# Two groups of attention heads as one pipeline beside a block-wise projection, with a new block order

## The chip, the cores and the metric

The kernel runs on one core of one Trainium2 chip. The metric is device time in microseconds (us), smaller is better. A core has TensorE (PE in the profile; PEld is its weight load), VectorE (DVE), ScalarE (ACT), GpSimd (POOL) and SyncE (SP), which issues the DMAs here. The program hands each engine a queue of instructions.

## The reference, cut to what matters

One step of a two-layer backbone on 1152 tokens (9 tiles of 128: tile 0 is the context, tiles 1 to 8 are latent). The even layer, of which the changed part computes the inputs and one branch:

```python
def even_layer(x, shift, scale, gate, norm_pre, norm_post, w_out, w_in, sink, ..., ctx):
    h = rms_norm(x, norm_pre) * (1.0 + scale) + shift
    qa, ka, va, ga, pb, gb = split_cols(h @ w_in, [...])
    ya = gqa_window_latent(apply_rope(qa), apply_rope(ka), va, k_ctx, v_ctx, sink)   # mixer A
    yb, _ = rwkv_mix(pb, ...)                                                        # mixer B
    y = concat([ya * silu(ga), yb * silu(gb)]) @ w_out
    return x + gate * rms_norm(y, norm_post)
```

Mixer A has two groups of four query heads that share one key and value head. A latent tile attends to the 128 cached context tokens and to a window of itself and the tile on either side, with a sink in the softmax; the context tile attends to itself alone. The odd layer (differential attention) follows and is not touched.

## The kernel before

**Phase 1** computes the modulation and the normed input, split into a high and a low part (`hh`, `hl`), and then runs two generators beside each other. Phase 2 runs mixer B's scan and everything after it.

**The fill** (`transposed`, L517) computes the other projections in transposed form, 128 output columns a block, in the order of the list `blocks` (L715). Kind `a` is mixer A's gate (4 blocks), `b` mixer B's inputs (13), `g` mixer B's gate (4). A block is three thirds of 24 matmuls of 128x384 (`ps<-hh,wgh`, `ps<-hl,wgh`, `ps<-hh,wgl`, L368 to L370): 72 a block, 1512 in all. "Fill matmul n" counts these. A third ends in a PSUM bank that is copied out. For `b` (`b_block`) ACT copies it into `bo` (L467, L468; two buffers). After the third third POOL adds the neighbours of `bo` into `bs`, ACT and DVE form `bm` (L473, L474), and `bm` is stored to `pbT` (L477, L478). There is one `bs` and one `bm`. Blocks b4 to b7 (the keys) put two more steps on a list that is worked off one step a third: `norms` (ones matmuls on `bs`, L493, and from them `yb`) and `scale` (transposes of `yb` on PE, L508; DVE scales `bm`, L512; a second store). Block b12 puts two `low_rank` steps there: store, two loads of `bo<-pbT` back, ACT's cast into `bs` (L421), DVE's remainder, a store.

**Mixer A** (`a_group`, L543) takes one group `g`: weights `wa`, cached keys and values, then nine tiles. Tile t has `project` (24 matmuls, L354 to L356, `ps<-wah,hh` and so on; rotary; values split into `vh`, `vl`), `turn` (5 transposes, L575 and L578, to `kst` and `qs`), twice `probs` (four heads, two at a time) and `values`. `probs` makes scores `s` (L601, mask L604) in the only score tile in PSUM, then DVE takes the maximum (L608), ACT the exponentials into `p` (L614) and DVE scales `p` (L619); `p` has two buffers. `values` transposes `p` (L632), ACT and DVE split it (`ph` L634, `pl` L635), and PE accumulates `po` (L643 to L645). Steps overlap over tiles: in round k the kernel projects tile k, does the values of k-2, turns k and does the probabilities of k-1. The generator `mixer_a` runs group 0 to its end and then group 1, so that a pipeline of nine tiles drains and another begins. The caches' keys and values sit in slot 0 of `kst`, `vh`, `vl`.

**The order.** `run(rest, 56, mixer_a(), 2 * (4 * NT + 2 * NT - 2))` zips the two generators (56 steps of the one against 104 of the other). The code stands in a block opened by `tc.block(schedule_with_timeline_sim=True)`, whose planner lays the instructions of every engine out anew from planned times and priorities, from the start to the first steps of phase 2. So the queues follow neither the code nor the list alone.

Of the kernel before, what the change touches and what calls it, by code (L numbers as in the profile page):

```python
# [19 lines left out]
P = 128  # L20
# [121 lines left out]
def hybrid_step(ctx: ExitStack, tc: tile.TileContext, I, O, stop=99):  # L142
# [315 lines left out]
    def b_block(i, w, later, pool, psum, p_tr, hh, hl, ind):  # L458
# [29 lines left out]
        yb = tl(pool, [P, 2 * NT, 64], "yb", bufs=1)  # L488
# [54 lines left out]
    def a_group(g, hh, hl, wp, rp, ap, psum, rope, idb, msk):  # L543
# [6 lines left out]
        kr, vr = tl(ap, [P, P], "kr"), tl(ap, [P, 64], "vr")  # L550
        SP.dma_start(kr, I["akT"][g])
        SP.dma_start(vr, I["av"][:, g])
        stack_split(kst[:, 0:P], kr)
        dup_split(vh[:, 0], vl[:, 0], vr)
        kp, vph, vpl = (tl(ap, [P, P], n, F32R) for n in ("kp", "vph", "vpl"))
        qks, qss, prs = {}, {}, {}

        def project(t):
            ps = tl(p_pr, [P, 512], "ps")
            proj_nat(ps, hh, hl, wh, wl, t, THIRD)  # L560
            qk = qks[t] = tl(ap, [P, 5, 2, 64], "qk", bufs=2)
            rope_apply(ap, rope, ps, 5, None if t == 0 else t - 1, [qk])
            if t == 0:
                v = tl(ap, [P, 64], "vn")
                VE.tensor_copy(v, ps[:, 320:384])
                SP.dma_start(O["ak"][:, g], qk[:, 4, 0])
                SP.dma_start(O["av"][:, g], v)
                dup_split(vph, vpl, v)
            else:
                dup_split(vh[:, t], vl[:, t], ps[:, 320:384])  # L570

        def turn(t):
            qk = qks.pop(t)
            pq, pk = tl(p_tr, [P, 512], "pt"), tl(p_tr, [P, 512], "pt")
            PE.transpose(pk[:, :P], qk[:, 4].rearrange("p o d -> p (o d)"), ident)  # L575
            stack_split(kp if t == 0 else kst[:, P * t:P * t + P], pk[:, :P])
            for r in range(4):
                PE.transpose(pq[:, P * r:P * r + P], qk[:, r].rearrange("p o d -> p (o d)"), ident)  # L578
            qs = qss[t] = tl(ap, [P, 2, 512], "qs", F32R, bufs=2)
# [3 lines left out]
        def near(t):  # L583

            if t == 0:
                return [(0, kp)], [(vph, vpl)], []
            lo, hi = max(1, t - 1), min(8, t + 1)
            kv = [(vh[:, j], vl[:, j]) for j in [0] + list(range(lo, hi + 1))]
            return ([(0, kst[:, 0:P]), (P, kst[:, P * lo:P * hi + P])], kv,
                    ([(P, 0)] if t > 1 else []) + ([(P * len(kv) - P, 1)] if t < 8 else []))  # L590

        def probs(t, hp):
            runs, kv, masks = near(t)
            nk = P * len(kv)
            qs = qss[t]
# [16 lines left out]
            p = prs[t, hp] = tl(ap, [P, 2, 512], "p", bufs=2)  # L612
# [8 lines left out]
        def values(t):  # L621
            kv = near(t)[1]
            pr = [prs.pop((t, hp)) for hp in range(2)]
# [32 lines left out]
        for k in range(NT + 2):  # L656
            if k < NT:
                project(k)
                yield
            if 2 <= k:  # L660
                yield from values(k - 2)
            if k < NT:
                turn(k)
                yield
            if 1 <= k <= NT:
                for hp in range(2):
                    probs(k - 1, hp)
                    yield
# [5 lines left out]
    blk.__enter__()  # L674
    with ExitStack() as ph1:
# [25 lines left out]
        left, right, rope = load_cst(bp, "left", "right", "rope")  # L701
# [1124 lines left out]
```

## Time and profile before

| | us |
|---|---|
| median of 3 runs | 2173.63 (2169.96 to 2176.01) |
| profiled execution | 2174.75 |
| its span | 2173.0 |
| PE busy in the span | 2004.3 (92%) |
| PE busy from 408 to 550 | 142.0 of 142.0 |
| PE busy from 550.44, after the fill's last matmul, to 564.70 | 8.40 of 14.26 |
| PE busy from 564.70 to 589.10, mixer A's last result | 18.45 of 24.40 |

The mean clock of TensorE that was granted over the span is 0.968 of full speed. Times in the views count from the start of the span. A row of a timeline has the start, the length, the engine, the line of the kernel, the operation, the tiles written and read and, in brackets, how long the engine stood idle before it and what released it. `PEclk` and the clock of a stretch are shares of the full speed of 2.4 GHz, and 0.5 is the lower level of 1.2 GHz.

### The profile page before, as it was taken

What the parts mean: (1) busy time and instruction counts of PE and PEld (TensorE: products, weight loads), DVE (VectorE), ACT (ScalarE), POOL (GpSimd) and SP (SyncE); (2) the same over time, 40 slices, a digit from 0 to 9 for tenths busy, and PEclk for the clock granted to TensorE, in tenths of its full rate; (3) what the DMA queues carried; (4) which work ended last, traced back from release to release, by engine and by line L of the source; (5) the groups of instructions that cost most, each with busy time, mean ns of one, the idle gap of its engine ahead of it and who ended that gap; (6) DMA issues with size and microseconds to landing.
All of it is one profiled execution on the core that took longest, in us unless ns stands there. A gap on an engine that the chain in (4) does not pass through costs nothing. (4 is left out here: it accounts for less than half of the span.)

```text
span 2173.0 us, 40867 instructions
## 1 busy us (share of the span) xinstructions
PE 2004.3 (92%) x15258; PEld 1780.6 (82%) x15258; DVE 1466.5 (67%) x3650; ACT 1070.9 (49%) x2856; POOL 668.4 (31%) x933
## 2 busy tenths in 40 slices
PE   6899998999688898988998889999999999999998
PEld 4899997999566777776776779899999999898786
DVE  3445546544565686868648758778788888887867
ACT  3433343433345455555436555555555555555643
POOL 0222132221046555665405311321212222222204
PEclk9999999999888999999999999999999999999999
DMA  7321221311354454543466440100010010101315
GB/s 285 122 86 62 83 76 58 106 52 43 99 181 129 127 170 139 172 131 115 137 193 216 151 124 5 53 28 30 27 30 28 29 30 28 34 23 47 96 58 182
DMA packets 164935, 205.73 MB, mean 95 GB/s; under 512 B 16352, under 2 KB 107904, under 8 KB 164736
## 3 DMA queue, kind: packets, MB, share of 16 engines
q1 hardware_dynamic: 161872, 198.25, 28.9%
q10 hardware_dynamic: 2864, 4.85, 0.7%
q8 instruction: 121, 1.98, 0.4%
q14 instruction: 78, 0.64, 0.1%
HBM read 152.32 MB, written 50.74 MB: 93 GB/s over the span
## 5 line engine op out<-in xcount | busy, mean ns | idle before, releaser
L1501 ACT ACTIVATE p<-s,mx 128x384 f32<-128x384 f32 (+1 forms) x400 | 225.1, 572 | 127.8 <-DVE mx L1498 106.9
L1496 DVE TENSOR_REDUCE mc<-s 128x1 f32<-128x384 f32 x384 | 205.1, 552 | 29.2 <-PE s L1494 25.8
L354 PE MATMUL ps<-wch,hh 128*128 128x384 f32 x576 | 205.7, 358 | 7.5 <-DVE hh L1645 6.1
L1494 PE MATMUL s<-kst,qs 128*128 128x384 f32 x768 | 197.0, 355 | 11.6 <-ACT p L1501 11.0
L355 PE MATMUL ps<-wcl,hh 128*128 128x384 f32 x576 | 198.9, 345 | 4.5 <-POOL wcl L263 4.5
L356 PE MATMUL ps<-wch,hl 128*128 128x384 f32 x576 | 197.2, 342 | 2.1 <-DVE hl L1646 2.0
L401 POOL TENSOR_TENSOR q<-ropea,ropeb 128x256 f32<-128x256 f32 x56 | 43.1, 769 | 450.0 <-DVE ropeb L398 322.8
L368 PE MATMUL ps<-hh,wgh 128*128 128x384 f32 x504 | 174.7, 347 | 6.3 <-DVE bo L234 6.3
L369 PE MATMUL ps<-hl,wgh 128*128 128x384 f32 x504 | 173.8, 345 | 0.0
L370 PE MATMUL ps<-hh,wgl 128*128 128x384 f32 x504 | 172.9, 343 | 0.0
L263 POOL TENSOR_TENSOR wgl<-raw,wgh 128x1024 fp32r<-128x1024 f32 (+1 forms) x39 | 75.1, 1929 | 293.6 <-ACT wgh L262 278.2
L1494 PEld LDWEIGHTS s<-kst,qs 128*128 128x128 f32 x768 | 127.0, 189 | 29.6 <-ACT p L1501 20.9
L1031 POOL TENSOR_TENSOR tmp<-mp,rp 128x126 f32<-128x126 f32 (+22 forms) x279 | 132.1, 473 | 53.3 <-DVE mp L1024 28.3
L1033 POOL TENSOR_TENSOR rp<-rp,tmp 128x126 f32<-128x126 f32 (+22 forms) x279 | 127.7, 458 | 21.9
L1377 ACT CAST ah<-pt 128x512 fp32r<-128x512 f32 (+2 forms) x168 | 86.2, 534 | 81.8 <-PE pt L1532 79.5
L1378 DVE TENSOR_TENSOR al<-pt,ah 128x512 fp32r<-128x512 f32 (+2 forms) x168 | 100.8, 616 | 33.7 <-ACT ah L1377 32.3
L354 PEld LDWEIGHTS ps<-wch,hh 128*128 128x128 f32 x576 | 110.4, 192 | 13.3 <-issue 3.4
L355 PEld LDWEIGHTS ps<-wcl,hh 128*128 128x128 f32 x576 | 110.2, 191 | 7.6 <-POOL wcl L263 7.2
L356 PEld LDWEIGHTS ps<-wch,hl 128*128 128x128 f32 x576 | 109.8, 191 | 3.9 <-DVE hl L1646 3.8
L368 PEld LDWEIGHTS ps<-hh,wgh 128*128 128x128 f32 x504 | 96.4, 191 | 8.2 <-DVE bo L234 6.9
L1532 PE MATMUL pt<-cst,p 128*128 128x128 f32 x584 | 95.2, 277 | 5.7 <-DVE p L1514 4.7
L1514 DVE SCALAR_TENSOR_TENSOR p<-p,lr,p 128x1152 f32<-128x1152 f32 (+1 forms) x72 | 99.8, 1386 | 0.3
(462 smaller groups left out, 5676.8 us busy)
## 6 DMA issues: line engine op xcount, KB each, us to landing
hb<-pbT SPq DMA_DIRECT2D x90, 256.0 KB, 4.2
adaw<-in_ada_w_dram SPq DMA_DIRECT2D x64, 256.0 KB, 3.5
raw<-in_wc_dram SPq DMA_DIRECT2D x48, 256.0 KB, 2.8
adaw<-in_ada_w_dram SPq DMA_DIRECT2D x8, 1024.0 KB, 11.7
pbT<-bm SPq DMA_DIRECT2D x16, 512.0 KB, 2.7
low<-lowT SPq DMA_DIRECT2D x16, 512.0 KB, 4.9
raw<-in_wo_dram SPq DMA_DIRECT2D x32, 256.0 KB, 2.8
raw<-in_wpb_dram SPq DMA_DIRECT2D x13, 512.0 KB, 3.6
```

What stands on the lines that cost most here:

```text
L354: PE.matmul(ps[:, :n], hh[:, k, s], wh[:, k], start=k == 0, stop=False)
L355: PE.matmul(ps[:, :n], hh[:, k, s], wl[:, k], start=False, stop=False)
L356: PE.matmul(ps[:, :n], hl[:, k, s], wh[:, k], start=False, stop=k == KT - 1)
L368: PE.matmul(ps[:, :THIRD], wh[:, k], hh[:, k, s], start=k == 0, stop=False)
L369: PE.matmul(ps[:, :THIRD], wh[:, k], hl[:, k, s], start=False, stop=False)
L370: PE.matmul(ps[:, :THIRD], wl[:, k], hh[:, k, s], start=False, stop=k == KT - 1)
L1031: eng.tensor_tensor(tv, mp[:, j:j + 1, 0:j].to_broadcast([P, n, j]), rpb[:, t:16, j:j + 1].to_broadcast([P, n, j]), ALU.mult)
L1033: eng.tensor_tensor(rpb[:, t:16, 0:j], rpb[:, t:16, 0:j], tv, ALU.add)
L1378: VE.tensor_tensor(lo, src, hi.bitcast(F32), ALU.subtract)
L1494: PE.matmul(s[c][:, :w], qs[:, e, z], hd.kp[:, z] if own else hd.kst[:, z, w * c:w * c + w], start=e == 0, stop=e == 1)
L1496: VE.tensor_reduce(mc[:, c:c + 1] if nb > 1 else mx, s[c][:, :w], axis=AX.X, op=ALU.min)
L1501: AE.activation(e[:, w * c:w * c + w], s[c][:, :w], AF.Exp, scale=-1.0, bias=mx, accum_out=sums[:, z, c:c + 1])
```

## The change

`mixer_a` is one function over u = 0 to 17, with g, t = divmod(u, 9). Round k projects tile k, does the values of k-2, turns k and does the probabilities of k-1 over both groups, so that group 1's first tile is projected while group 0's last tiles are still in the pipeline. For that, the context's own keys and values (`own`) and the cached ones (`cache`) are tiles apart from `kst`, `vh`, `vl`, with two buffers each, and `begin(1)` loads group 1's weights and cache after the projection of u = 8; `wa` still has one buffer. `hurried` wraps every step of mixer A in a raised priority of 1000 for the planner. The zip is 56 steps against 108. `p` has three buffers. `yb` lies in `bs` (`s[:, :TOK]`) and not in a tile of its own. The masks are loaded through one of the two raw buffers of the weights. The order of the blocks is new: gate blocks stand between b4, b5, b6 and b7, and b12 comes right after b0.

```diff
+    def hurried(work, n):
+        while True:
+            with tc.high_priority(n):
+                if next(work, 0) == 0:
+                    return
+            yield
...
-        yb = tl(pool, [P, 2 * NT, 64], "yb", bufs=1)
+        yb = s[:, :TOK].rearrange("p (n t) -> p n t", t=64)
...
-    def a_group(g, hh, hl, wp, rp, ap, psum, rope, idb, msk):
+    def mixer_a(hh, hl, wp, rp, ap, psum, rope, idb, msk):
-        wh, wl = weights(wp, I["wa"][g], THIRD, "wa", rp, bufs=1)
-        kst = tl(ap, [P, TOK], "kst", F32R)
-        vh, vl = tl(ap, [P, NT, P], "vh", F32R), tl(ap, [P, NT, P], "vl", F32R)
+        kst = tl(ap, [P, TOK - P], "kst", F32R)
+        vh, vl = tl(ap, [P, NT - 1, P], "vh", F32R), tl(ap, [P, NT - 1, P], "vl", F32R)
+        own, cache, ws = {}, {}, {}
...
+        def begin(g):
+            ws[g] = weights(wp, I["wa"][g], THIRD, "wa", rp, bufs=1)
+            kr, vr = tl(ap, [P, P], "kr"), tl(ap, [P, 64], "vr")
+            SP.dma_start(kr, I["akT"][g])
+            SP.dma_start(vr, I["av"][:, g])
+            own[g], cache[g] = ([tl(ap, [P, P], n + e, F32R, bufs=2) for n in ("k", "vh", "vl")] for e in "pc")
+            stack_split(cache[g][0], kr)
+            dup_split(*cache[g][1:], vr)
...
+            if t == NT - 1 and g == 0:
+                begin(1)
...
-            p = prs[t, hp] = tl(ap, [P, 2, 512], "p", bufs=2)
+            p = prs[u, hp] = tl(ap, [P, 2, 512], "p", bufs=3)
...
-        for k in range(NT + 2):
-            if k < NT:
+        for k in range(2 * NT + 2):
+            if k < 2 * NT:
...
+    sys_blocks = "a0 a1 b4 a2 b5 a3 b6 g0 b7 g1 b0 b12 b8 b1 b2 b3 b9 b10 b11 g2 g3"
...
-        left, right, rope = load_cst(bp, "left", "right", "rope")
+        rope, = load_cst(bp, "rope")
...
-        for i, n in enumerate((left, right)):
-            VE.tensor_copy(msk[i], n)
+        sides = tl(rp, [P, 1024], "raw")
+        SP.dma_start(sides[:, :2 * P], I["cst"][:, CST["left"][0]:sum(CST["right"])])
+        for i in range(2):
+            VE.tensor_copy(msk[i], sides[:, P * i:P * i + P])
...
-        blocks = [("a", 0), ("a", 1)] + [("b", i) for i in (4, 0, 5, 1, 6)] + [("a", 2), ("a", 3)] + [
-            ("b", i) for i in (7, 2, 3, 12, 8, 9, 10, 11)] + [("g", i) for i in range(4)]
+        blocks = [(n[0], int(n[1:])) for n in sys_blocks.split()]
-        run(rest, 56, mixer_a(), 2 * (4 * NT + 2 * NT - 2))
+        run(rest, 56, hurried(mixer_a(hh, hl, wp, rp, ap, psum, rope, idb, msk), 1000), 12 * NT * 1)
```

How PE's queue reads at two places and ACT's at one follows. In the names, `ps` is the bank of a projection, `s` a score tile, `pt` a bank for transposes, `po` the accumulated values; the number behind a name is the buffer.

PE, group 0's last tile (t = 8), first pair of heads, before: the end of its score tile and what stands behind it.

```order
L604 MATMUL s_3188<-msk_158_665,idb_664 128x128
L632 MATMUL pt_3076<-cst_61,p_3013 128x128
L632 MATMUL pt_3085<-cst_61,p_3013 128x128
L632 MATMUL pt_3097<-cst_61,p_3013 128x128
L632 MATMUL pt_3076<-cst_61,p_3013 128x128
L632 MATMUL pt_3085<-cst_61,p_3013 128x128
L632 MATMUL pt_3097<-cst_61,p_3013 128x128
L643 MATMUL po_3073<-ph_3081,vh_955 128x512
```

The same place now (line numbers of the changed kernel: L654 are the transposes of `p`, L376 to L378 the fill):

```order
L625 MATMUL s_3256<-msk_158_665,idb_664 128x128
L654 MATMUL pt_3124<-cst_61,p_3055 128x128
L654 MATMUL pt_3133<-cst_61,p_3055 128x128
L654 MATMUL pt_3145<-cst_61,p_3055 128x128
L654 MATMUL pt_3124<-cst_61,p_3055 128x128
L654 MATMUL pt_3133<-cst_61,p_3055 128x128
L654 MATMUL pt_3145<-cst_61,p_3055 128x128
L376 MATMUL ps_3366<-hh_96,wgh_2972 128x384
L377 MATMUL ps_3366<-hl_97,wgh_2972 128x384
L378 MATMUL ps_3366<-hh_96,wgl_2973 128x384
```

Before, mixer A's work from the second score tile of t = 7 to the first two products of the values of t = 8 stands in one piece behind fill matmul 888, with no fill matmul in it; now 25 fill matmuls stand between the six transposes and the next score tile.

PE behind fill matmul 1512, the last, before:

```order
L370 MATMUL ps_5426<-hh_96,wgl_5018 128x384
L601 MATMUL s_5235<-kst_3346,qs_4986 128x128
L632 MATMUL pt_5144<-cst_61,p_5072 128x128
L632 MATMUL pt_5153<-cst_61,p_5072 128x128
L632 MATMUL pt_5165<-cst_61,p_5072 128x128
L632 MATMUL pt_5144<-cst_61,p_5072 128x128
L632 MATMUL pt_5153<-cst_61,p_5072 128x128
L632 MATMUL pt_5165<-cst_61,p_5072 128x128
L643 MATMUL po_5141<-ph_5149,vh_3347 128x512
```

And now:

```order
L378 MATMUL ps_5494<-hh_96,wgl_5134 128x384
L622 MATMUL s_5235<-kc_2825,qs_4929 128x128
L622 MATMUL s_5235<-kst_942,qs_4929 128x384
L622 MATMUL s_5235<-kc_2825,qs_4929 128x128
L622 MATMUL s_5235<-kst_942,qs_4929 128x384
```

Before, the values of group 1's tile 6, the turn of tile 8 and both score tiles of tile 7 are still to come behind the last fill matmul; now the second score tile of tile 7 is the first piece behind it, and what follows is the same as before from there.

ACT around the first low-rank cast of block b12 (`bs<-bo`), before:

```order
L468 COPY bo_3629<-ps_3699 128x384
L421 CAST bs_3695<-bo_3692 128x1152
L614 ACTIVATE p_3743,li_3738<-s_3725,mx_3736 128x384 x2
L468 COPY bo_3629<-ps_3784 128x384
L611 ACTIVATE sm_3737<-sm_3737 128x2
```

And now (L656 is `ph`, L600 `qs`, L434 the split of the values, L476 the copy of a fill bank):

```order
L429 CAST bs_3512<-bo_3509 128x1152
L656 CAST ph_3421<-pt_3416 128x512
L429 CAST kst_942<-pt_3476 128x128
L600 CAST qs_3484<-pt_3475 128x512
L434 CAST vh_943<-ps_3561 128x128
L476 COPY bo_3445<-ps_3516 128x384
```

Before, the exponentials of a score tile stand behind the cast; now a cast of `ph`, the copies of keys and queries, the split of values and the copy of a fill bank do.

## Rows read from the trace of the kernel before

**Rows 1.** Page, first part: engine, busy time, share of the span, instructions.

```profile
PE 2004.3 (92%) x15258; PEld 1780.6 (82%) x15258; DVE 1466.5 (67%) x3650; ACT 1070.9 (49%) x2856; POOL 668.4 (31%) x933
```

**Rows 2.** Stretches: length, busy (instructions) PE, PEld, DVE, ACT, POOL; clock, DMA share, GB/s.

```profile
286.00:290.00 4.00, 2.47 (x16) 2.13 (x16) 3.16 (x5) 1.78 (x5) 1.84 (x2) 1.00 0.49 131
316.00:342.00 26.00, 23.43 (x152) 22.12 (x151) 14.03 (x36) 9.18 (x20) 6.06 (x3) 1.00 0.11 34
342.00:360.00 18.00, 13.15 (x66) 10.15 (x67) 13.53 (x32) 8.22 (x24) 0.94 (x3) 0.80 0.14 48
360.00:363.00 3.00, 3.00 (x11) 3.00 (x11) 0.43 (x1) 1.23 (x2) 1.30 (x1) 0.51 0.50 195
384.00:408.00 24.00, 21.93 (x128) 21.28 (x127) 10.70 (x25) 10.17 (x25) 5.19 (x4) 0.93 0.55 156
408.00:550.00 142.00, 142.00 (x871) 136.80 (x870) 68.67 (x146) 48.69 (x113) 30.76 (x18) 1.00 0.15 50
550.44:564.70 14.26, 8.40 (x40) 6.29 (x39) 7.10 (x16) 5.13 (x13) 2.16 (x8) 0.87 0.81 239
564.70:589.10 24.40, 18.45 (x81) 14.04 (x81) 13.94 (x34) 8.04 (x23) 0.00 (x0) 0.73 0.04 11
```

**Rows 3.** PE timeline, 286 to 360: start, length, instruction [idle before <-releaser].

```profile
288.18 0.55 PE L632 MATMUL pt<-cst,p 128*128 128x128 f32 x3 [1.13 <-DVE p L619]
...
342.24 1.04 PE L601 MATMUL s<-kst,qs 128*128 128x128 f32 x4 [2.81 <-ACT p L614]
...
353.60 0.44 PE L632 MATMUL pt<-cst,p 128*128 128x128 f32 x2 [1.21 <-DVE bm L512]
356.83 1.54 PE L632 MATMUL pt<-cst,p 128*128 128x128 f32 x6 [2.79 <-DVE p L619]
...
359.70 0.60 PE L368 MATMUL ps<-hh,wgh 128*128 128x384 f32 x1
```

**Rows 4.** Timeline, 352 to 360, block b7 (DVE, DMA issue SPq, ACT).

```profile
352.93 0.61 DVE L512 SCALAR_TENSOR_TENSOR bm<-bm,prm,pt 128x384 f32<-128x384 f32 x1
...
353.57 0.33 SPq L478 DMA_DIRECT2D pbT<-bm  x1
...
356.33 1.26 ACT L473 ACTIVATE bm<-bo,mu 128x1154 f32<-128x1154 f32 x1 [0.40 <-issue]
...
359.00 0.28 ACT L467 COPY bo<-ps 128x128 f32<-128x128 f32 x1
```

**Rows 5.** Timelines of ACT and PE around block b12's low-rank cast.

```profile
393.22 1.15 ACT L421 CAST bs<-bo 128x1152 fp32r<-128x1152 f32 x1 [5.83 <-DMA bo<-pbT]
397.93 0.58 ACT L614 ACTIVATE p<-s,mx 128x384 f32<-128x384 f32 x1 [3.56 <-DVE mx L609]
...
399.22 0.72 PE L601 MATMUL s<-kst,qs 128*128 128x128 f32 x4 [2.07 <-ACT p L614]
```

**Rows 6.** Timeline of PE after the fill's last matmul.

```profile
550.26 0.34 PE L370 MATMUL ps<-hh,wgl 128*128 128x384 f32 x1
...
561.37 0.28 PE L604 MATMUL s<-msk,idb 128*128 128x128 bf16 x2
564.70 1.43 PE L601 MATMUL s<-kst,qs 128*128 128x128 f32 x4 [3.05 <-ACT p L614]
...
570.84 1.22 PE L601 MATMUL s<-kst,qs 128*128 128x128 f32 x4 [1.77 <-ACT p L614]
...
584.09 0.90 PE L632 MATMUL pt<-cst,p 128*128 128x128 f32 x6 [3.19 <-DVE p L619]
...
588.69 0.40 PE L645 MATMUL po<-pl,vh 128*128 128x512 f32 x1
590.08 0.69 PE L905 MATMUL py<-low,lora 128*128 128x512 f32 x2 [1.00 <-PE po L645]
```

**Rows 7.** Timeline of the start, ACT and PE.

```profile
30.06 1.04 ACT L262 CAST wgh<-raw 128x1024 fp32r<-128x1024 f32 x1 [0.22 <-DMA raw<-in_wga_dram]
...
34.17 1.86 PE L289 MATMUL ps<-adaw,sc 128*2 128x128 f32 x8 [8.76 <-DVE x L334]
```

More of the change, by code (lines that the diff above doesn't have):

```diff
@@ L541, in transposed, with project @@
                 f()
-    def a_group(g, hh, hl, wp, rp, ap, psum, rope, idb, msk):
+    def mixer_a(hh, hl, wp, rp, ap, psum, rope, idb, msk):
         p_pr, p_tr, p_s, p_o = psum
-        wh, wl = weights(wp, I["wa"][g], THIRD, "wa", rp, bufs=1)
-        kst = tl(ap, [P, TOK], "kst", F32R)
-        vh, vl = tl(ap, [P, NT, P], "vh", F32R), tl(ap, [P, NT, P], "vl", F32R)
[L550 to L555, printed above, removed]
-        qks, qss, prs = {}, {}, {}
-        def project(t):
+        kst = tl(ap, [P, TOK - P], "kst", F32R)
+        vh, vl = tl(ap, [P, NT - 1, P], "vh", F32R), tl(ap, [P, NT - 1, P], "vl", F32R)
+        own, cache, ws = {}, {}, {}
+        qks, qss, prs = {}, {}, {}
+        def begin(g):
[6 more added lines that the diff above has]
+            dup_split(*cache[g][1:], vr)
+        def project(u):
+            g, t = divmod(u, NT)
+            if t == 0 and g not in ws:
+                begin(g)
+            wh, wl = ws[g]
+            kp, vph, vpl = own[g]
             ps = tl(p_pr, [P, 512], "ps")
             proj_nat(ps, hh, hl, wh, wl, t, THIRD)
-            qk = qks[t] = tl(ap, [P, 5, 2, 64], "qk", bufs=2)
+            qk = qks[u] = tl(ap, [P, 5, 2, 64], "qk", bufs=2)
             rope_apply(ap, rope, ps, 5, None if t == 0 else t - 1, [qk])
@@ L569, in project, with turn, near, probs @@
             else:
-                dup_split(vh[:, t], vl[:, t], ps[:, 320:384])
-        def turn(t):
-            qk = qks.pop(t)
+                dup_split(vh[:, t - 1], vl[:, t - 1], ps[:, 320:384])
+            if t == NT - 1 and g == 0:
+                begin(1)
+        def turn(u):
+            g, t = divmod(u, NT)
+            qk = qks.pop(u)
             pq, pk = tl(p_tr, [P, 512], "pt"), tl(p_tr, [P, 512], "pt")
             PE.transpose(pk[:, :P], qk[:, 4].rearrange("p o d -> p (o d)"), ident)
-            stack_split(kp if t == 0 else kst[:, P * t:P * t + P], pk[:, :P])
+            stack_split(own[g][0] if t == 0 else kst[:, P * t - P:P * t], pk[:, :P])
             for r in range(4):
                 PE.transpose(pq[:, P * r:P * r + P], qk[:, r].rearrange("p o d -> p (o d)"), ident)
-            qs = qss[t] = tl(ap, [P, 2, 512], "qs", F32R, bufs=2)
+            qs = qss[u] = tl(ap, [P, 2, 512], "qs", F32R, bufs=2)
             AE.copy(qs[:, 0], pq)
             VE.tensor_tensor(qs[:, 1], pq, qs[:, 0].bitcast(F32), ALU.subtract)
-        def near(t):
+        def near(u):
+            g, t = divmod(u, NT)
             if t == 0:
-                return [(0, kp)], [(vph, vpl)], []
+                return [(0, own[g][0])], [own[g][1:]], []
             lo, hi = max(1, t - 1), min(8, t + 1)
-            kv = [(vh[:, j], vl[:, j]) for j in [0] + list(range(lo, hi + 1))]
-            return ([(0, kst[:, 0:P]), (P, kst[:, P * lo:P * hi + P])], kv,
+            kv = [cache[g][1:]] + [(vh[:, j - 1], vl[:, j - 1]) for j in range(lo, hi + 1)]
+            return ([(0, cache[g][0]), (P, kst[:, P * lo - P:P * hi])], kv,
                     ([(P, 0)] if t > 1 else []) + ([(P * len(kv) - P, 1)] if t < 8 else []))
-        def probs(t, hp):
-            runs, kv, masks = near(t)
+        def probs(u, hp):
+            runs, kv, masks = near(u)
             nk = P * len(kv)
-            qs = qss[t]
+            qs, g = qss[u], u // NT
             s = tl(p_s, [P, 2, 512], "s")
@@ L619, in probs, with values @@
                 VE.tensor_scalar(p[:, r, :nk], p[:, r, :nk], li[:, r:r + 1], None, op0=ALU.mult)
-        def values(t):
-            kv = near(t)[1]
-            pr = [prs.pop((t, hp)) for hp in range(2)]
+        def values(u):
+            g, t = divmod(u, NT)
+            kv = near(u)[1]
+            pr = [prs.pop((u, hp)) for hp in range(2)]
             po = tl(p_o, [P, 512], "po")
@@ L661, in a_group @@
                 yield from values(k - 2)
-            if k < NT:
+            if k < 2 * NT:
                 turn(k)
                 yield
-            if 1 <= k <= NT:
+            if 1 <= k <= 2 * NT:
                 for hp in range(2):
@@ L707, in hybrid_step @@
         VE.tensor_copy(idb, ident)
-        for i, n in enumerate((left, right)):
-            VE.tensor_copy(msk[i], n)
-        def mixer_a():
-            for g in range(2):
-                yield from a_group(g, hh, hl, wp, rp, ap, psum, rope, idb, msk)
-        blocks = [("a", 0), ("a", 1)] + [("b", i) for i in (4, 0, 5, 1, 6)] + [("a", 2), ("a", 3)] + [
-            ("b", i) for i in (7, 2, 3, 12, 8, 9, 10, 11)] + [("g", i) for i in range(4)]
+        sides = tl(rp, [P, 1024], "raw")
[3 more added lines that the diff above has]
+        blocks = [(n[0], int(n[1:])) for n in sys_blocks.split()]
         rest = transposed(blocks, wp, rp, bp, psum[0], psum[1], hh, hl, ind)
         run(some(rest, 7), 1, None, 1)
-        run(rest, 56, mixer_a(), 2 * (4 * NT + 2 * NT - 2))
+        run(rest, 56, hurried(mixer_a(hh, hl, wp, rp, ap, psum, rope, idb, msk), 1000), 12 * NT * 1)
     if stop <= 1:
```

## The prediction, made before the changed kernel ran

> **What bounds the kernel now.** I read the busy shares first: PE is busy 92% of the span and no other engine over 67% [rows 1]. The mean hides which stretches are full, so I went to PE's busy time by stretch. From 408 to 550 it is busy 142.0 of 142.0 us at full clock [rows 2]: there mixer A's waits are filled by projection matmuls, and nothing that lets another engine go faster can gain. Time is to be had only where PE is not full. In phase 1, behind the first 100 us, these are the stretches 286 to 290, 316 to 363 (the change from group 0 to group 1), 384 to 408 (block b12's low-rank step) and 550.44 to 589.10 (the end of mixer A, the fill being used up) [rows 2]. Then I read PE's timeline in each for what ended the idle time [rows 3, 5, 6]: nearly always the softmax, ACT's exponentials (L614) ahead of the next score tile, or DVE's scaling (L619) ahead of the transposes. The reader should see a chain, score, maximum, exponentials, scaling, transposes, that is late only when PE has nothing else in its queue. After 589.10 phase 2 starts with a matmul on PE, 1.00 us behind mixer A's last `po` [rows 6], and the queues from there on read as before. So phase 2 moves as a block, and what phase 1 saves is saved at the end. The change has no instructions fewer to speak of: the same 1512 fill matmuls and 18 tiles. It can gain idle time and low clock only.
>
> **Part 1, the change of groups (316 to 363).** Before, the queue has no fill matmul behind number 888 until mixer A is through with tile 7. Idle time: 26.00 - 23.43 = 2.57 and 18.00 - 13.15 = 4.85, together 7.42 us [rows 2]; the large pieces are 2.81, 1.21 and 2.79 [rows 3]. Clock: 0.80 over 18.0 us means 7.2 us at the lower level; PE is busy 73% of that stretch, so 5.3 us of work at half speed, 2.6 us lost. From 360 to 363, clock 0.51, another 3.0 us of work, 1.5 lost. Between 286 and 290 the same wait on L619 costs 1.53 [rows 2, 3]. Sum: 7.42 + 2.6 + 1.5 + 1.53 = 13.0; with every low-clock microsecond counted as work, 10.2 / 2 = 5.1 in place of 4.1, so 14.0.
>
> Why the fill stopped is the second half of this. Block b7 is followed by another `b` block, and there is one `bm`: b7's scaling ends at 353.54, its store is issued at 353.57, the next block's L473 starts at 356.33, and the first copy into a free `bo` at 359.00; PE takes up the fill at 359.70 [rows 3, 4]. The chain from b7's scaling to that copy is about 6 us (353.54 to 359.00), and the fill waits for all of it. In the new list every one of b4 to b7 is followed by a gate block, which needs no `bm`. In the new queue b7's scaling stands at fill matmul 832, and the copy that needs the next `bo` (block b8's) behind number 888. That is 56 matmuls, at the dense stretch's 142.0 / 871 = 0.163 us each [rows 2] 9.1 us, and mixer A's matmuls between them, against 6 us needed. So the fill is there, and the quoted queue shows it behind the score tile of t = 8: 25 matmuls, some 4.1 us, for a chain that takes 3.05 us in the clear (561.65, the end of a score tile, to 564.70, the start of the next [rows 6]). I take 13.5 gained; ends 11 (one new wait of the size of 2.8 in it) and 15 (that the small gaps under 0.3 us go too).
>
> **Part 2, the end of mixer A.** Before, from the last fill matmul to 589.10 are 38.7 us: 14.26 with 8.40 busy at clock 0.87 and 24.40 with 18.45 busy at 0.73 [rows 2]. With A ahead of the fill in the planner, the work of the first 14.26 us now stands among fill matmuls, and the queue behind number 1512 begins with the score tile that ran at 564.70. That work still has to be done there: 8.40 us busy at clock 0.87 are 7.3 at full clock, and its 40 instructions at the dense stretch's 0.163 us are 6.5. So the first piece gives 14.26 - 7.3 = 7.0 to 14.26 - 6.5 = 7.8. The second piece stays, but it now comes straight behind full-speed fill: the score tile that took 1.43 a half at the low level [rows 6] starts at full clock. At 0.73, 54% of 24.40 us is low, 13.2 us, of which 76% is work, 10.0, so 5.0 lost; I count half of it as saved, 2.5, from 0 to 5. Sum: 7.5 + 2.5 = 10, ends 7 and 12.8.
>
> **Part 3, the low-rank step.** Before, ACT stood 5.83 us for `bo<-pbT` ahead of the cast at 393.22, the exponentials queued behind it came at 397.93, and PE lost 2.07 at 399.22 [rows 5] and 24 x 0.14 / 2 = 1.7 to the clock, 3.8 us in all [rows 2]. Now the cast stands ahead of more: a `ph`, the copies of keys and queries, a fill bank's copy. PE has fill matmuls in its own queue there too, as before, so I take about 4 us again and a change of 0, from -3.8 (nothing waits) to +8 (two casts that hold PE as long as ACT stood, 11.7, less the 3.8). The row shows an engine that stands for one transfer while ready work is queued behind. The Trainium skill says the same as a rule, that ACT, DVE and GpSimd are strict FIFO (Perfetto Trace Analysis, section on the Tensor Engine Instruction); it speaks against this change, which puts A's copies behind that cast, and taken at its worst it gives rival 1.
>
> **Part 4, small edits.** `yb` in `bs` holds `bs` until the scaling has read it, but `bm` is held to that point and past it already, so 0. The cached keys' own tiles and the mask's load: two small casts and one small DMA among the first. PE's longest early idle time, 8.76 us to 34.17, and the first weight cast at 30.06 [rows 7] sit behind the same DMA queue, in which one weight load moves behind the modulation's loads; I take -0.5, from -1 to +2. A fill third in the new queue (at number 1273) takes a bank straight behind the third that held it, with no matmul in between: the nearest row is the copy at 359.00, behind which PE goes on at 359.70 [rows 3, 4], 0.7 us without the way from PE to ACT, so +1 once, from 0 to 1.5. Four of the score tiles in the middle now have 2.6 to 3.5 us of other work behind them, against 3.05 in the clear and 2.07 more where the exponentials were late [rows 5]; half of them late by 1 us is +2, from 0 to 8 (all four by 2.07).
>
> **Sum.** -13.5 - 10 + 0 - 0.5 + 1 + 2 = -21.0 us. Against the profiled execution's own 2174.75 (the span of 2173.0 and 1.75 around it): 2153.7; that run lies 1.1 above the median of 2173.63, so 2152.6 as a median. I say 2153.
>
> **Rivals.**
> 1. The queue behind the low-rank casts (part 3 at its worst) and the shorter cover of the scores give part of it back: two casts that hold PE 5.8 us each and some 3 us of low clock, 14.6 in place of the 3.8 of before, so 11 us back: 2164. For it: the rows of 393 to 399. Against it: PE lost 2.07 before, not 5.83, and that is all the idle time from 384 to 408 [rows 2], so the second cast held nothing.
> 2. Slower. The fill stops behind `b` blocks again, now at more places: b6, b7 and b0 each need the one `bs` and `bm` while the key block ahead has still to be scaled. Each such stop costs what the one of before did, about 13 us; three of them add 39: 2192; from two on, 2179, the change loses. What decides is whether PE reaches a copy into a new `bo` within some 6 us of the scaling ahead. Against it: 56 fill matmuls for b7 and more for b5 and b6.
> 3. The change doesn't do what it says at the end: mixer A is still as far behind when the fill ends, because its own chain and not its priority sets its pace. Then part 2 gives nothing: 2163. Against it: the queue behind number 1512 begins later in A's work, whatever the pace.
> 4. More: the third `p` takes the gaps at the end away. The gaps of 3.05, 1.77 and 3.19 [rows 6] repeat with each tile. The Trainium skill reads consistent bubbles as a possible lack of buffers for the next tile (Perfetto Trace Analysis, section Optimization Strategy). As a mechanism of this kernel: without those 8.0 us and with the other half of the clock's 5.0, the end is 10.5 shorter still, 2142. Against it: the releaser of 3.05 and 1.77 is the exponential that reads the score tile, of which there is still one, and that of 3.19 is DVE's scaling itself; no row names a `p` that wasn't free.
>
> **How the numbers follow.** Forecast (2146 to 2160) 0.66; rival 1 0.13; rival 2 0.05; rival 3 0.07; rival 4 0.09. The range leaves out rival 2 and the far half of rivals 1 and 4: 2139 to 2166. About 0.3%, 6.5 us, is what a measurement of this kernel can tell from no change, so faster means below 2167: the forecast, rival 4 and most of rivals 1 and 3 give 0.91; the same 0.05; slower 0.04, rival 2 for the most part.
>
> **What would show it.** Part 1: PE busy without a gap of 2 us from 316 on through the change of groups, and clock 1.00 there. Part 2: some 20 to 24 us from the last fill matmul to the first L905-like matmul of phase 2 (38.7 + 1.0 before), with the 3.05 and 3.19 still in it. Part 3: one ACT cast with a DMA named ahead of it, and 2 to 4 us idle on PE behind it. Phase 2 as long as before to within 3 us. Wrong would be a new gap of over 5 us between fill matmuls, or an end of mixer A as long as before.

## The result and the profile after

| | before | after |
|---|---|---|
| median | 2174.82 (2169.96 to 2177.91, 4 runs) | 2150.20 (2148.71 to 2152.83, 4 runs) |
| profiled execution, its span | 2174.75, 2173.0 | 2149.71, 2147.9 |
| first fill matmul | 55.14 | 53.98 |
| first projection of mixer A | 105.06 | 104.18 |
| end of the fill's last matmul | 550.60 | 543.88 |
| end of mixer A's last `po` | 589.08 | 565.17 |
| phase 2's first matmul on PE, to the end of the span | 1582.9 | 1581.8 |

The ratio is 0.989, interval 0.9869 to 0.9912: 24.6 us, 1.1%. The span shrank by 25.1 us, of which 23.9 lie ahead of phase 2's first matmul (590.08 before, 566.16 after). Phase 2 moved as a block.

The page's busy line of the changed kernel (answers to [rows 1]):

```profile
PE 1993.3 (93%) x15258; PEld 1776.4 (83%) x15258; DVE 1453.3 (68%) x3650; ACT 1069.4 (50%) x2856; POOL 665.9 (31%) x933
```

PE did as many matmuls in fewer microseconds: its mean granted clock is 0.972 in place of 0.968. The changed kernel's busy time by stretch, columns as in [rows 2], at the same times up to 408 and then by its own events:

```profile
316.00:342.00 26.00, 26.00 (x172) 24.86 (x171) 17.31 (x44) 13.09 (x30) 5.83 (x5) 1.00 0.17 60
342.00:360.00 18.00, 18.00 (x111) 17.05 (x110) 11.32 (x28) 8.36 (x26) 2.44 (x2) 1.00 0.43 111
360.00:363.00 3.00, 1.52 (x8) 0.87 (x7) 2.92 (x7) 0.65 (x3) 0.21 (x1) 1.00 0.56 194
384.00:408.00 24.00, 24.00 (x150) 23.11 (x149) 11.76 (x25) 7.70 (x17) 7.72 (x6) 1.00 0.17 58
408.00:543.50 135.50, 134.85 (x820) 128.77 (x819) 67.29 (x135) 51.32 (x117) 29.15 (x20) 1.00 0.14 48
543.88:565.17 21.29, 15.51 (x81) 12.02 (x80) 13.93 (x35) 8.59 (x24) 2.70 (x8) 0.84 0.52 161
```

Where before had 7.42 us idle and a clock of 0.80, PE is busy 26.00 of 26.00 and 18.00 of 18.00 at full clock. The end is 21.29 us long in place of 38.5, at clock 0.84. PE's timeline of the changed kernel, columns as in [rows 3]: all its idle pieces of 0.8 us or more from 300 us to phase 2, with the fill's last matmul (L376 to L378 are now the fill, L622 the scores, L654 the transposes of `p`, L665 to L667 `po`):

```profile
361.42 0.50 PE L667 MATMUL po<-pl,vh 128*128 128x512 f32 x1 [0.90 <-DVE pl L657]
...
363.44 0.45 PE L376 MATMUL ps<-hh,wgh 128*128 128x384 f32 x1 [1.03 <-ACT bo L476]
```

```profile
543.54 0.34 PE L378 MATMUL ps<-hh,wgl 128*128 128x384 f32 x1
...
549.20 0.33 PE L622 MATMUL s<-kc,qs 128*128 128x128 f32 x1 [3.21 <-ACT p L635]
...
560.25 1.42 PE L654 MATMUL pt<-cst,p 128*128 128x128 f32 x6 [2.01 <-DVE p L640]
...
564.78 0.39 PE L667 MATMUL po<-pl,vh 128*128 128x512 f32 x1
566.16 1.17 PE L925 MATMUL py<-low,lora 128*128 128x512 f32 x4 [1.00 <-PE po L667]
```

The waits of [rows 3] and 2.07 of [rows 5] are gone. Of those at the end [rows 6], one score wait (3.21) and one wait on the scaling (2.01 in place of 3.19) are left. The first two pieces above belong to the low-rank step, whose first cast on ACT reads now:

```profile
358.10 1.16 ACT L429 CAST bs<-bo 128x1152 fp32r<-128x1152 f32 x1 [3.02 <-DMA bo<-pbT]
```

ACT stands 3.02 us for the same transfer (5.83 before, [rows 5]), and PE loses 0.90 + 1.03 us behind it. The way from the cast to PE leads over DVE, whose remainder of the low-rank step (L422 before, L430 now) needs the cast. DVE before, then now:

```profile
394.41 1.36 DVE L422 TENSOR_TENSOR bs<-bo,bs 64x1152 fp32r<-64x1152 f32 x1 [7.78 <-ACT bs L421]
395.80 0.96 DVE L608 TENSOR_REDUCE mx<-s 128x2 f32<-128x768 f32 x1
```

```profile
359.29 1.35 DVE L430 TENSOR_TENSOR bs<-bo,bs 64x1152 fp32r<-64x1152 f32 x1 [3.30 <-ACT bs L429]
360.67 0.69 DVE L657 TENSOR_TENSOR pl<-pt,ph 128x512 fp32r<-128x512 f32 x1
```

Before, a score tile's maximum stands behind the remainder, and the exponentials wait for that maximum ([rows 5]: 3.56, DVE). Now it is `pl`, for which PE waits the 0.90.

### The profile page after: what moved, and what is told of

It reads as the page before. It is cut to its first block, busy times and chain, and to the rows that moved or that the text cites. A ratio compares the mean times of both kernels' runs of the same rounds, so it can differ in the third digit from the quotient of the medians.

```text
span 2147.9 us, 40864 instructions
## 1 busy us (share of the span) xinstructions
PE 1993.3 (93%) x15258; PEld 1776.4 (83%) x15258; DVE 1453.3 (68%) x3650; ACT 1069.4 (50%) x2856; POOL 665.9 (31%) x933
## 5 line engine op out<-in xcount | busy, mean ns | idle before, releaser
L376 PE MATMUL ps<-hh,wgh 128*128 128x384 f32 x504 | 174.2, 346 | 8.4 <-DVE bo L242 6.6
L378 PE MATMUL ps<-hh,wgl 128*128 128x384 f32 x504 | 171.3, 340 | 0.0
L1053 POOL TENSOR_TENSOR rp<-rp,tmp 128x126 f32<-128x126 f32 (+22 forms) x279 | 131.8, 472 | 21.9
L376 PEld LDWEIGHTS ps<-hh,wgh 128*128 128x128 f32 x504 | 95.4, 189 | 10.4 <-DVE bo L242 7.1
L271 POOL TENSOR_TENSOR wcl<-raw,wch 128x512 fp32r<-128x512 f32 x54 | 74.0, 1379 | 83.2 <-ACT wch L270 83.1
```

Source lines behind the costliest of these rows:

```text
L271: eng.tensor_tensor(lo[:, j:j + w], raw[:, :w], hi[:, j:j + w].bitcast(F32), ALU.subtract)
L376: PE.matmul(ps[:, :THIRD], wh[:, k], hh[:, k, s], start=k == 0, stop=False)
L378: PE.matmul(ps[:, :THIRD], wl[:, k], hh[:, k, s], start=False, stop=k == KT - 1)
L1053: eng.tensor_tensor(rpb[:, t:16, 0:j], rpb[:, t:16, 0:j], tv, ALU.add)
```

## The experiments

The last fill matmul, mixer A's last `po` and phase 2's first matmul are read from each profile; the ratio is against the kernel before in the same comparison. "Middle" is PE's idle time from 100 us to the last fill matmul.

| kernel | ratio (95% interval) | last fill | last `po` | phase 2 | middle |
|---|---|---|---|---|---|
| before | 1 | 550.60 | 589.08 | 590.08 | 11.6 |
| changed | 0.9890 (0.9869 to 0.9912) | 543.88 | 565.17 | 566.16 | 5.1 |
| e1, old blocks | 0.9892 (0.9858 to 0.9925) | 549.05 | 569.30 | 570.29 | 8.1 |
| e2, no priority | 0.9988 (0.9972 to 1.0003) | 568.72 | 587.26 | 588.26 | 19.3 |
| e3, before + blocks | 0.9981 (0.9962 to 0.9999) | 549.27 | 583.42 | 584.42 | 13.0 |
| e4, before + blocks + priority | 0.9959 (0.9941 to 0.9976) | 549.09 | 584.40 | 585.40 | 8.2 |
| e5, small edits undone | 0.9917 (0.9896 to 0.9939) | 545.07 | 569.47 | 570.46 | 4.6 |
| e6, zip 1.6 | 0.9963 (0.9952 to 0.9975) | 569.46 | 570.16 | 576.58 | 13.3 |
| e7, zip 2.0 | 1.0178 (1.0156 to 1.0199) | 619.42 | 570.13 | 626.51 | 42.0 |
| e9, priority on probabilities | 0.9997 (0.9984 to 1.0010) | 564.60 | 586.22 | 587.22 | 17.1 |
| e10, priority on projections | 1.0039 (1.0020 to 1.0058) | 543.56 | 594.48 | 595.47 | 12.1 |
| e11, two `p` | 0.9973 (0.9954 to 0.9993) | 555.29 | 582.23 | 583.22 | 4.9 |
| e12, before + third `p` | 1.0029 (1.0015 to 1.0043) | 564.58 | 597.94 | 598.94 | 13.4 |
| e13, before + priority | 0.9952 (0.9933 to 0.9971) | 541.46 | 577.48 | 578.48 | 6.6 |

The times of single profiles and the ratios don't agree to the microsecond, because phase 2, which none of this touches on purpose, took from 1574.8 us (e10) to 1589.2 us (e6, which starts it otherwise) from its first matmul on.

### Which of the parts makes the gain

**e1**, the changed kernel with the list of before.

```diff
-    sys_blocks = "a0 a1 b4 a2 b5 a3 b6 g0 b7 g1 b0 b12 b8 b1 b2 b3 b9 b10 b11 g2 g3"
+    sys_blocks = "a0 a1 b4 b0 b5 b1 b6 a2 a3 b7 b2 b3 b12 b8 b9 b10 b11 g0 g1 g2 g3"
```

> The changed kernel with the old order of the fill's blocks. Theory (the one pipeline and its place in the queue make the gain, the block order little): its queue has no stretch without fill at the change of groups (the projections of tiles 9 and 10 of the pipeline stand at fill matmuls 692 and 763) and some 9 us of dense work behind the last fill matmul, so 2150 within 5 us, and the change of groups shows no gap over 1.5 us. Rival A (the order of blocks makes part 1, since b7 is followed by another b block again): a stop of the fill behind b7 returns, 10 to 13 us: 2160 to 2164, with a wait on L520's bm or on a bo copy of over 2 us.

Measured: 2151.42, ratio 0.9892, the same as the changed kernel's. No stop behind b7 came back (PE's longest idle piece from 300 to 480 us is 0.75). Rival A falls: with the pipeline and the priority in place, the block order is not what keeps the fill going. At the end of phase 1 it is worth some 4 us in these profiles (570.29 against 566.16): fill matmuls wait 2.40 and 2.27 us for DVE to write a gate (`bo`, L242) where gate blocks stand behind each other.

**e2**, the changed kernel without priority.

```diff
-        run(rest, 56, hurried(mixer_a(...), 1000), 12 * NT * 1)
+        run(rest, 56, hurried(mixer_a(...), 0), 12 * NT * 1)
```

> The changed kernel with the raised priority set to 0. Theory: one pipeline beside the fill is enough; its queue leaves about 9 us of dense work behind the last fill matmul, against 11 with the priority, and projections stand in single matmuls among the fill: 2150 within 6 us. Rival B (the priority makes the gain): mixer A falls behind, both the change of groups and the end wait again: 2165 or more.

Measured: 2174.3, ratio 0.9988. My theory fell here: one pipeline alone gains nothing that can be told, though less is left behind the last fill matmul (18.5 us from there to the last `po`, where the changed kernel takes 21.3). The loss is in the middle. What PE waited for from 100 us to the last fill matmul (engine, line, releaser: total, times, longest), e2 first, then the changed kernel:

```profile
PE s L622 <- ACT p L635: 9.8, 7, 3.6
PE pt L654 <- DVE p L640: 5.1, 6, 1.9
```

```profile
PE s L622 <- ACT p L635: 1.0, 1, 1.0
```

Seven score waits and six on the scaling of `p`, against one score wait and none on the scaling. Over the 36 score tiles, from the end of a tile's last matmul to the end of L640's second row, the scaled probabilities came 6.56 us later on the mean and 14.50 at most; with the priority 4.89 and 7.62; before, 5.42 and 11.14.

**e3**, before with the new list (the diff is the mirror of e1's), and **e4**, the same with the priority and the zip of 56 against 108, mixer A still in two runs; **e13**, the priority and that zip with the old list.

```diff
-        run(rest, 56, mixer_a(), 2 * (4 * NT + 2 * NT - 2))
+        run(rest, 56, hurried(mixer_a(), 1000), 12 * NT)
```

> The kernel before with the new order of blocks alone. Theory: the queue still has the stretch without fill matmuls at the change of groups and 16.6 us of dense work behind the last fill matmul, so at most 5 us gained: 2169 to 2176. Rival A (block order): part 1 is gained, 10 to 13 us: 2161 to 2165.

> The kernel before (two groups, one after the other) with the new order of blocks, the raised priority and the zip of 56 against 108. Theory: the draining pipeline at the change of groups is still there (no projection of mixer A between fill matmuls 693 and 821), 15.5 us of dense work stand behind the last fill matmul: 2163 to 2172. Rival B (the priority with the blocks makes the gain, the one pipeline none): 2150 within 5 us.

> The kernel before with the raised priority and the zip of 56 against 108 alone (old blocks, two groups apart). If the priority by itself shortens mixer A's chain on all engines: the middle loses its stall, some 10 us less than before, 0.995 to 0.997, as with the new blocks (0.9959). If it needs the one pipeline: within 0.2% of before. In either case the end stays near 35 us, since 16 us of dense work stand behind the last fill matmul.

Measured: e3 2172.07, 0.9981; e4 2167.15, 0.9959; e13 2160.36, 0.9952. The list alone gives 0.2%, some 4 us, within the 5 that were expected, and not in the middle (13.0 us idle). The priority without the pipeline gives half of the gain: in e13 the middle falls from 11.6 to 6.6 us idle, the fill ends 9.1 us earlier (541.46), and the stall at the change of groups is gone although the groups still run one after the other (no idle piece of PE over 1.2 us from 300 us to the last fill matmul). The zip of 108 in place of 104 goes with it; no run has that alone. The end stays: 36.0 us, 35.3 in e4, against 38.5. PE there in e13 (L609 the scores, L640 the transposes), which is [rows 6] over again:

```profile
551.14 1.44 PE L609 MATMUL s<-kst,qs 128*128 128x128 f32 x4 [3.23 <-ACT p L622]
...
557.28 1.22 PE L609 MATMUL s<-kst,qs 128*128 128x128 f32 x4 [1.77 <-ACT p L622]
...
571.42 1.54 PE L640 MATMUL pt<-cst,p 128*128 128x128 f32 x6 [3.19 <-DVE p L627]
```

What the pipeline adds to the priority is read from e4 and e5 (below): both have the new list, the priority, the zip of 108, two buffers for `p` and `yb` in a tile of its own, and they differ in the one pipeline and its tiles alone. It takes the ratio from 0.9959 to 0.9917 and phase 2's first matmul from 585.40 to 570.46, of which the end is 10.9 us (35.3 against 24.4).

So the pipeline needs the priority, and the priority alone gives only half: it keeps the middle full, and the one pipeline, with it, lets the last tiles move in among the fill. Without the priority the pipeline pays in the middle what it saves at the end.

### What the priority works through

Both start from e2. **e9** puts the priority on the probabilities alone:

```diff
-                    probs(k - 1, hp)
+                    with tc.high_priority(1000):
+                        probs(k - 1, hp)
```

**e10** puts it on the projections alone:

```diff
-                project(k)
+                with tc.high_priority(1000):
+                    project(k)
```

> The changed kernel with the raised priority on the probabilities alone (scores, maximum, exponentials, scaling); projections, turns and values without it. Theory E (the priority works through the softmax chain on DVE and ACT, which then doesn't stand behind the fill's copies): the scaled probabilities come back near 4.9 us behind the scores' end on the mean, as with full priority, and idle time of PE from 100 us to the last fill matmul falls from 19.3 to 8 or less: 2158 or less. Theory F (it works through the projection, which without it is spread among the fill in single matmuls, so that both banks fill slowly and the tile comes late): idle time in the middle stays above 14 us, 2168 or more.

> The raised priority on the projections alone. Its queue has the projections in one piece again, but 24 us of dense work behind the last fill matmul. Theory E: scaled probabilities still 6 us or more behind the scores' end on the mean, middle above 14 us idle, and a longer end: 2175 or more. Theory F: the middle as good as with full priority (8 us idle or less), the end some 15 us longer: 2160 to 2170.

Measured: e9 2169.84, 0.9997, middle 17.1, probabilities 6.53 us behind the scores; e10 2181.42, 1.0039, middle 12.1, probabilities 5.57, and 50.9 us from the last fill matmul to the last `po`. Theory E falls: with the probabilities alone preferred, nothing comes back. Theory F is half right: with projections in one piece the probabilities are nearly as early as before and the middle is better, but not the 8 us that it asked for, and the rest of mixer A falls behind and waits at the end. So neither step carries it alone. Of what was tried, only the priority on all steps of mixer A gained (the changed kernel against e2, and e13 against before); the turns and values alone, and pairs of steps, were not tried.

### The end: what it is long for, and what it covers

**e6** has mixer A earlier still, and **e7** the same with 2 in place of 1.6.

```diff
-        run(rest, 56, hurried(mixer_a(...), 1000), 12 * NT * 1)
+        run(rest, 56, hurried(mixer_a(...), 1000), int(12 * NT * 1.6))
```

> The changed kernel with the zip at 56 against 172 (1.6 times 108), so that mixer A's queue ends with the fill: behind fill matmul 1512 stand 0.7 us of dense work in place of 11. Theory (the end is long only because nothing is left to fill it): the 21.3 us from the last fill matmul to the last po fall to 3 or less, of which 11 come back as work among the fill: 2139 to 2143. Rival D (mixer A's chain sets the pace): with 46 to 50 fill matmuls a tile in place of about 75 the score tiles wait in the middle, 36 of them by 0.3 us or more: 2150 or more.

> The same with 56 against 216 (2.0 times): mixer A ends some 600 fill matmuls ahead of the fill's end, with about 36 fill matmuls a tile. Theory: at most 3 us worse than the zip of 1.6, 2139 to 2146, and no idle time behind mixer A's last po. Rival D: waits in each of the 18 tiles, 2150 or more.

Measured: e6 2166.73, 0.9963; e7 2213.28, 1.0178. In e6 the end went as the theory said, from 21.29 to 0.70 us, and still the kernel got 16 us slower than the changed one. The time is rival D's. Busy time by stretch in e6, columns as in [rows 2]:

```profile
100.00:300.00 200.00, 193.28 (x1187) 185.26 (x1186) 96.38 (x236) 74.67 (x169) 48.10 (x31) 0.99 0.24 81
300.00:500.00 200.00, 193.47 (x1190) 183.14 (x1188) 108.98 (x253) 80.04 (x187) 45.28 (x38) 0.99 0.22 72
500.00:569.40 69.40, 69.40 (x426) 66.64 (x425) 31.35 (x64) 26.36 (x61) 13.69 (x8) 1.00 0.14 50
570.20:608.00 37.80, 23.67 (x210) 17.39 (x211) 23.07 (x46) 17.66 (x48) 4.41 (x12) 0.77 0.76 240
```

From 100 to 500 PE has 13.3 us idle and some low clock, where the changed kernel has 5.1 idle at full clock: some 47 fill matmuls stand from one projection to the next, in place of some 72 (tiles 2 to 17). PE's longest waits in e6 from 100 us to the last fill matmul (columns as in e2's):

```profile
PE pt L654 <- DVE bm L520: 3.1, 1, 3.1
PE s L622 <- ACT p L635: 2.2, 2, 1.3
PE ps L362 <- DVE vl L435: 1.8, 1, 1.8
PE ps L376 <- DVE vl L435: 1.6, 2, 1.2
```

So rival D is right that less fill a tile leaves PE idle in the middle (in e7 42.0 us), but not in where: two score tiles make PE wait 0.3 us or more, not 36, and most of the idle time is waiting for results of DVE. From 500 on PE is full again (69.40 of 69.40), since the projections are through by then and 290 fill matmuls stand among the last tiles. And the end had a use. The DMA issues in e6, with PE's first matmul of phase 2:

```profile
569.92 0.59 SPq L911 DMA_DIRECT2D low<-lowT  x1
570.56 0.61 SPq L916 DMA_DIRECT2D lora<-loraT  x1
```

```profile
576.58 2.04 PE L925 MATMUL py<-low,lora 128*128 128x512 f32 x4 [6.41 <-DMA lora<-loraT]
584.90 1.44 PE L1009 MATMUL pa<-zr,kbt 64*128 64x128 f32 x10 [6.28 <-DVE kbt L965]
```

and the same two issues in the changed kernel:

```profile
544.30 0.59 SPq L911 DMA_DIRECT2D low<-lowT  x1
544.94 0.60 SPq L916 DMA_DIRECT2D lora<-loraT  x1
```

Both kernels issue phase 2's first loads right behind the last fill matmul. In the changed kernel mixer A's last 21 us cover them; in e6 PE stands 6.41 us for `lora` and 6.28 for DVE. Phase 2's first matmul comes 10.4 us later than in the changed kernel, of which 5.0 are mixer A's later end. Not all of the waiting is new. Behind its first matmul the changed kernel stands for the next load, which in e6 lands during the wait for DVE:

```profile
572.32 2.05 PE L925 MATMUL py<-low,lora 128*128 128x512 f32 x4 [4.99 <-DMA lora<-loraT]
```

From the last `po` to the first matmul of the scan proper (`yb<-zr,S`, L1164, at 594.71 and in e6 at 608.64) it is 29.5 us in the changed kernel, 6.5 of them idle, and 38.5 in e6, 14.2 of them idle (clock 0.88 and 0.78): without the cover it takes 8.9 us more. e7, where mixer A is done 49 us ahead of the fill's end, stands 7.09 us for the same `lora`. e8, the same zip with the old list, gave no time: mixer A comes there to gate rows that blocks a2 and a3 have not written yet.

### The small edits, the third buffer, and where tiles lie

**e11** undoes the third buffer alone:

```diff
-            p = prs[u, hp] = tl(ap, [P, 2, 512], "p", bufs=3)
+            p = prs[u, hp] = tl(ap, [P, 2, 512], "p", bufs=2)
```

**e5** undoes it together with two more small edits:

```diff
-        yb = s[:, :TOK].rearrange("p (n t) -> p n t", t=64)
+        yb = tl(pool, [P, 2 * NT, 64], "yb", bufs=1)
...
-        rope, = load_cst(bp, "rope")
+        left, right, rope = load_cst(bp, "left", "right", "rope")
...
-        sides = tl(rp, [P, 1024], "raw")
-        SP.dma_start(sides[:, :2 * P], I["cst"][:, CST["left"][0]:sum(CST["right"])])
```

**e12** gives the kernel before a third buffer, with `yb` in `bs`:

```diff
-            p = prs[t, hp] = tl(ap, [P, 2, 512], "p", bufs=2)
+            p = prs[t, hp] = tl(ap, [P, 2, 512], "p", bufs=3)
...
-        yb = tl(pool, [P, 2 * NT, 64], "yb", bufs=1)
+        yb = s[:, :TOK].rearrange("p (n t) -> p n t", t=64)
```

> The changed kernel with three small edits undone: two buffers for p, yb in a tile of its own, the masks loaded in one tile with the rotary table. Theory: none of them stands on the path; the third p buffer is never the one waited for: 2150 within 4 us; the first fill matmul about 1 us later, as before (55.1 against 54.0), and that is all of it. Rival C (the third buffer carries part of the gain): waits of ACT's exponentials for a free p show again in the score chain, exponentials later than 3.5 us behind the scores' end on the mean, 2156 or more.

> The changed kernel with two buffers for p and nothing else undone. If the third buffer carries what the three small edits undone cost at the end (24.4 us from the last fill matmul to the last po, against 21.3): 24 us again, a wait of 3.19 on DVE's scaling in place of 2.01, 2153 to 2156. If it carries nothing: 21.3 and 2150 within 3 us, and the cost came from the masks' load and yb.

> The kernel before with a third buffer for p (and yb in bs, which makes the room). Its queue is the one of before: 16.6 us of dense work behind the last fill matmul and no fill at the change of groups. If the third buffer lets the exponentials of a tile start before the transposes of the one two ahead are done, the end of mixer A gets 3 to 5 us shorter (38.5 before), the last wait on DVE's scaling falls from 3.19 to about 2.0, and the wait at the change of groups by 1 to 2: 4 to 7 us less than before in the same comparison. If it is hidden there: within 2 us of before.

Measured: e5 2157.50, 0.9917; e11 2166.52, 0.9973; e12 2177.09, 1.0029. Two things are in these numbers.

*The third buffer works at the end.* From the last fill matmul to the last `po` are 21.29 us with three buffers and 24.40 (e5) and 26.94 (e11) with two; before, 38.48 with two and 33.36 (e12) with three. So 3.1 and 5.6 us in the changed kernel, 5.1 in the one of before; e11's clock there is lower than e5's (0.75 against 0.79), so that its 5.6 are not the buffer's alone. ACT's exponentials (L614 before, L635 after) of tile 8's first pair show it, before, then e5, then the changed kernel:

```profile
576.82 0.58 ACT L614 ACTIVATE p<-s,mx 128x384 f32<-128x384 f32 x1 [0.59 <-PE pt L632]
```

```profile
556.74 0.58 ACT L635 ACTIVATE p<-s,mx 128x384 f32<-128x384 f32 x1 [0.52 <-PE pt L654]
```

```profile
552.67 0.60 ACT L635 ACTIVATE p<-s,mx 128x384 f32<-128x384 f32 x1
```

With two buffers the exponentials are released by PE's transposes of the tile two ahead (0.59, 0.52); with three nothing is in their way. From the exponentials of the score tile ahead to these it is 7.85 us in e5 (from 548.89) and 4.97 in the changed kernel (from 547.70), which is 2.9 of the 3.1. The last wait on the scaling is 3.19 with two buffers, in e5, e11 and e13 as before, and 2.01 with three in the changed kernel and in e12 (1.58 in e1). The order has a part in that: with three buffers (changed, e12) PE's last score tile runs three `po` products earlier than with two (before, e5, e11), so what stands behind the last fill matmul is not quite the same as before. How much of the 1.2 us is order was not told apart. PE in e12:

```profile
593.92 0.88 PE L632 MATMUL pt<-cst,p 128*128 128x128 f32 x6 [2.01 <-DVE p L619]
```

*The layout moved.* In e11 and e12 the first fill matmul came at 78.01 and 76.71, not at 54 to 56. PE and SP in e12:

```profile
76.71 0.69 PE L368 MATMUL ps<-hh,wgh 128*128 128x384 f32 x1 [9.07 <-ACT wgh L262]
```

```profile
71.17 0.34 SPq L182 DMA_DIRECT2D cstones<-in_cst_dram  x1
71.56 0.42 SPq L261 DMA_DIRECT2D raw<-in_wga_dram  x1
```

In the kernel before the second of these, the first load of weights, was issued at 19.91. The setup's last tiles (`hf`, three of 1536 bytes a partition) end at byte 176000 of a partition. By the addresses in the compiled programs the tile of ones, which SP loads ahead of the first weights, begins at 175520 in e12 and at 173472 in e11, in the setup's memory, so that its load waits for the setup and SP's queue with it. SP's wait just ahead of that load in e12 (total, times, longest; L348 is the setup's last step that reads `hf`):

```profile
SPq L182 <- DVE hl L348: 9.8, 1, 9.8
```

In the kernel before it begins at 176032, in e5 at 179104, in the changed kernel at 177568: clear of the setup. Mixer A's first projection comes 11.4 us later in e12 and 12.4 in e11 (116.50 and 116.54). That is what makes e12 slower than before and most of what makes e11 worse than e5. So the times that were expected of e11 (2153 to 2156) and e12 (4 to 7 us less than before) did not come, while the last wait on the scaling did as expected in both (3.19 and 2.01). Of e5 the theory (2150 within 4 us) fell and rival C came: 2157.50, a wait of the exponentials for a free `p` (0.52), and exponentials that end 3.56 us behind the scores on the mean, against 3.09 in the changed kernel.

## Why the prediction was right, point by point

The forecast was 2153, range 2139 to 2166; 2150.2 was measured. In profiled spans it is -25.1 against -21.0.

- **Part 1** (13.5 gained, with 3 for part 4's new waits 10.5 net). From mixer A's first projection to the last fill matmul: 445.5 us before, 439.7 now, with the first piece of the old end moved in. By part 2's own price for that piece, 6.5 to 7.3, the middle gained 12 to 13, part 3's 1.9 among them. The size was right. The second half of the reason was not: the stop was put down to b7's chain and the new list was to cure it. e1 has the old list and no such stop, e3 the new list, 13.0 us idle in the middle and one piece of 6.32 at 370.79 (PE for DVE's scaling, L619), e13 the old list, the old pipeline and 6.6. The priority cured it (in e13 with the zip of 108). The prediction had read the priority from the queue only as part of the whole and gave it no term of its own.
- **Part 2** (10 gained). 38.5 - 21.3 = 17.2, less 6.5 to 7.3 moved: 9.9 to 10.7. Right in size. (The 550.44 of the rows lies inside the fill's last matmul, which ends at 550.60; hence 38.5 and not 38.7.) The second piece was to shrink from 24.40 to 21.9, and is 21.29, but the reason given, full clock at its start, was not enough by itself: e5, with the same 81 matmuls behind the last fill matmul and two `p`, needs 24.40 again, at clock 0.79 against 0.84. The third buffer makes that difference, so that the 2.5 us put down for the clock fit by luck.
- **Part 3** (0, from -3.8 to +8). PE lost 1.93 at full clock in place of 3.8: 1.9 gained. The term was some 2 us too dear; ACT stood 3.02 for the transfer and not 5.83. The way to PE was misread too: [rows 5] names DVE's maximum ahead of the exponentials, not the cast, so it was DVE's queue, not ACT's, that held up ready work (7.78 for the cast, above).
- **Part 4.** The start gained 1.2 by the first fill matmul (0.5 forecast). Score tiles with short cover: one wait of 1.03 us (at 232) where 2 was put down; fill matmul 1273 waited 0.57 for its bank where 1 was put down. No wait of PE over 0.3 us up to the last fill matmul names `yb` or `bs`; no run undoes that edit alone. What the step missed is that these edits also place the tiles: e11 and e12 lose 11 to 12 us at the start because the tile of ones lies 4096 and 512 bytes lower.
- The 4.1 us beyond the forecast are 1.5 to 2.5 from the middle, 1.1 from phase 2, 0.4 from the start and the rest from the end.
- **Rival 1** did not come: 1.93 behind the first cast, nothing behind the second. **Rival 2** did not: no wait of a fill matmul over 1.03 from 100 us to the last. **Rival 3** did not come to the changed kernel, but shows where an edit is missing: without the priority (e2) or without the one pipeline (e13) the gain is nothing or half.
- **Rival 4** was dismissed with "no row names a `p` that wasn't free". That was wrong: ACT's row at 576.82 above does, with 0.59 us, and I had looked only at PE's. Its mechanism was true for some 3 us, not for 10.5, since the score tile's own wait stays (3.21). These 3 us are the ones that part 2 had put down to the clock.

## What to carry to other kernels

Where a planner lays out the queues, ask of each edit what it does alone and what it does with the others: here one pipeline (with the list and the third buffer) gained 0.1%, not to be told from nothing, the priority (with the new zip) 0.5%, and all together 1.1%; step by step it is 0.2% with the list (e3), 0.4% with the priority (e4), 0.8% with the pipeline (e5) and 1.1% with the third buffer and the other small edits. A stretch that waits on one engine may cover something on another: before filling it, list what is issued at its start and when that lands (here phase 2's loads, for which PE stood 6.4 us once the cover was gone, 8.9 us in all). And when a buffer is added or taken away, see that the first loads are still issued as early as before; who waits for a buffer is read on the engine that writes it, not on the one that reads the result.

## What the runs showed of the hardware

TensorE's granted clock differs between runs of one and the same program, and the time with it: e1's runs are 2147.96 us at a mean clock of 0.976 and 2160.77 at 0.968, and the kernel before in that comparison lies between 2167.36 (0.970) and 2182.59 (0.962). That is 13 to 15 us, more than most of the steps that were to be told apart here.
